# A decoder trunk whose MLPs use seven block products: engine work and weight sums in another order

## Chip, cores, metric

One core of one Trainium2 chip runs the whole program in one launch. The metric is device time in microseconds, the median of several executions. One further execution is profiled; rows and durations below come from that one.

## What is computed

The reference is a trunk of two blocks over 1040 tokens (16 meta tokens and 1024 real ones), width 1024, float32: differential attention, then gated linear attention, each followed by a squared-ReLU MLP with 4096 hidden units. The change touches the MLPs alone:

```python
def sq_relu_mlp(x, w_up, w_down):
    return jnp.square(jax.nn.relu(x @ w_up)) @ w_down
...
for i in range(DEPTH):
    hn = rmsnorm(h, mix_norm_w[i])
    ...
    h = h + sq_relu_mlp(rmsnorm(h, mlp_norm_w[i]), mlp_w_up[i], mlp_w_down[i])
return rmsnorm(h[:, N_META:], final_norm_w)
```

## The kernel before, in words

Activations lie with features on partitions and tokens along the free axis. A product in float32 accuracy is made of three fp32r matmuls: each operand is split into a high part (a CAST on ACT, line 229) and a low part (a subtraction on DVE, line 230, `split_to`), and high x high, low x high and high x low are summed in PSUM.

Each MLP matrix product is done as a 2 x 2 block product with seven instead of eight block multiplications (numbered 1 to 7) and sums of operand blocks. In layer 0 a token half has 520 columns and takes two PSUM banks of 260; in layer 1 it has 512 columns in one bank.

**The first MLP product** (`mlp`, line 941) goes through 16 steps p of 256 hidden units. For each p two 512 KB tiles of weights (`raw`, line 681) hold the blocks A11, A12 and A21, A22. `sums` (line 961) forms on POOL S1 = A21 + A22 in a tile of the pool "tmp" (line 966), then at once S2 = S1 - A11, S3 = A22 - S2, S4 = A12 - S2 in place (lines 969 to 971). `wop_next` (line 974) splits one weight operand into the next of 11 tiles used in a ring; seven operands are ahead of the product in hand. `product` issues a product's matmuls (`part`, line 1000), 24 of 260 columns in layer 0, 12 of 512 columns in layer 1, in the order 1(p), 4(p-1), 2(p), 3(p-1), 6(p), 5(p), 7(p). Products 1, 6, 7 and 4 of one p add up in one bank group without clearing it, so after each of them `after` (line 1052) has to read the banks: ACT copies after 1, 6 and 7 (lines 1059, 1061, 1063), DVE reads after 4. Bank groups alternate with p. So the copy after 7(p) must be done when 4(p) begins, one product later. `gate` (line 1031) applies relu times the norm's factor on DVE (line 1033) and squares on ACT (line 1034). After product 3, `spill_pair` (line 1036) forms T1 to T4 (DVE, lines 1040 to 1048, tiles of "tmp", which has four buffers) and writes seven operands of the second product to DRAM (`xd`).

**The second MLP product** (`Down`, line 725) takes the seven block products in the order `DORD` = 5, 3, 1, 6, 7, 4, 2, each in 16 steps kp; within a step its four output parts mp take turns (`mul`, line 866; matmul line 872). `make_w` (line 788) loads the weight blocks (line 767), sums them (lines 806, 809 and 816 on POOL, 811 on DVE) and splits them; `make_x` reads `xd` back (line 840) and splits it. The first four of these reads land in "tmp". At a product's last kp `evict` (line 876) adds each bank to the residual tile `hacc` on DVE (line 880). `hacc` is loaded during product 5 (line 898). Layer 0 uses banks 2 mp and 2 mp + 1 for all products; layer 1 uses bank mp for 5, 3 and bank mp + 4 for 1, 6, 7, 4.

The engines' queues are not in the order of the code: the framework's scheduler puts an instruction into its engine's queue when its own model has it ready, and uses the code's order as a priority; each engine then works through its queue in order and waits there on semaphores.

Of the kernel before, what the change touches and what calls it, by code (L numbers as in the profile page):

```python
# [8 lines left out]
F32 = mybir.dt.float32  # L9
# [41 lines left out]
def tile_hybrid_trunk(ctx, tc, hT, win, lamp, wout, gwin, gwz, gwup, gwout, wup, wdn, wdl,  # L51
# [676 lines left out]
    class Down:  # L728
        def __init__(self, layer, op, cfg, xd, hook):
            self.__dict__.update(locals())  # L730
            self.tw, self.ns = cfg.tw, len(cfg.subs)
            self.half = (slice(0, cfg.tw), slice(cfg.tw, 2 * cfg.tw))
            self.acc, self.S, self.W, self.X, self.R, self.st = {}, {}, {}, {}, {}, {}
            self.nr = self.nw = self.nx = self.nd = 0
            self.rawp, self.wp, self.stage = [], 1, None
# [8 lines left out]
            self.xring = list(cfg.os[11:16]) + list(cfg.os[7:11]) + list(cfg.os[:7])  # L744
# [42 lines left out]

        def make_w(self, upto):
            while self.nw < min(upto, len(self.wseq)):
                n = self.nw  # L790
                it = self.wseq[n]
                i = it[0]
                j = it[1] if len(it) == 2 else 4 * it[1] + it[2]
                nr = self.rneed(n)
                self.raw(nr)
                at = self.w_place(n)
                if at is None:
                    self.wp = 1 - self.wp
                    o = wpool.tile([P, KT * P], F32R, tag=("wh", "wl")[self.wp], name=nm("wop"))
                else:  # L800
                    o = slot(at, "wop", F32R, (P, KT * P))
                if i == 5:
                    if j % 2 == 0:
                        self.S[j // 2] = slot(self.cfg.ops[j // 2], "S", F32, (P, 2, 512))
                    src = self.S[j // 2][:, j % 2, :]
                    nc.gpsimd.tensor_add(src, self.raw_of(5, j, "A21"), self.raw_of(5, j, "A22"))  # L806
                elif i == 3:
                    S = self.S[j // 2][:, j % 2, :]
                    nc.gpsimd.tensor_sub(S, S, self.raw_of(3, j, "A11"))
                    src = self.raw_of(3, j, "A12")  # L810
                    nc.vector.tensor_sub(src, src, S)  # L811
                elif i == 6:
                    src = self.S[j // 2][:, j % 2, :]
                elif i == 7:
                    src = self.raw_of(7, j, "A22")
                    nc.gpsimd.tensor_sub(src, src, self.S[j // 2][:, j % 2, :])
# [14 lines left out]
        def dma_x(self, upto):  # L831
            while self.nd < min(upto, 112):
                i, kp = self.xseq[self.nd]
                if self.nd < 4:
                    t = tmp("xr")[:, :self.tw]
                else:
                    if self.stage is None:
                        self.stage = [slot(self.cfg.ops[14 + q], "xr", F32, (P, 2, self.tw)) for q in range(2)]
                    t = self.stage[self.nd // 2 % 2][:, self.nd % 2, :]
                nc.sync.dma_start(t, self.xd[i][kp])  # L840
                self.X[i, kp] = t
                self.nd += 1

        def make_x(self, upto):
            tw = self.tw
            while self.nx < min(upto, 112):
                i, kp = self.xseq[self.nx]
                self.dma_x(self.nx + 1)
                o = slot(self.xring[self.nx % 16], "xop", F32R, (P, 2 * tw))
                split_to(o[:, :tw], o[:, tw:], self.X[i, kp])  # L850
                self.X[i, kp] = o
                self.nx += 1
                if self.nx >= 4 or self.nd < 4:
                    self.dma_x(min(self.nx + 2, 4) if self.nx < 4 else self.nx + 2)
# [20 lines left out]

        def evict(self, i, mp, c0, b, nb, n):
            e, h = INTO[i]
            m = 4 * (1 - e) + mp
            a = self.acc[m][:, h * self.tw + c0:h * self.tw + c0 + nb * n].rearrange("p (s n) -> p s n", s=nb)
            nc.vector.tensor_add(a, PS[:, b:b + nb, :n], a)  # L880

        def run(self):
            ns, subs = self.ns, self.cfg.subs
            t = 0
            for i in DORD[:6]:
                par = 1 if i in (1, 6, 7, 4) else 0
                for kp in range(NP2):
                    self.make_w(t + 6 if t < 72 else t + 4 if t < 92 or ns == 2 else 98 + 2 * (t - 92))
                    self.make_x(t + 6 if t < 80 else t + 6 + (t - 79) // 2)
                    for mp in range(4):  # L890
                        b = 2 * mp if ns == 2 else mp + 4 * par
                        self.mul(i, kp, mp, subs, range(b, b + ns), i in (3, 6, 7, 4))
                        if kp == NP2 - 1:
                            self.evict(i, mp, 0, b, ns, subs[0][1])
                    if i == 5 and 3 <= kp < 11:
                        m = kp - 3
                        self.acc[m] = slot(self.cfg.acc[m], "hacc")
                        nc.sync.dma_start(self.acc[m][:, :2 * self.tw], self.op.hm[m])
                    self.hook(self, i, kp)
                    t += 1  # L900
            if ns == 2:
                for mp in range(4):
                    for kp in range(NP2):
# [4 lines left out]
                        self.mul(2, kp, mp, subs, (2 * mp, 2 * mp + 1), False)  # L908
                        if kp == NP2 - 1:
                            self.evict(2, mp, 0, 2 * mp, 2, subs[0][1])  # L910
                        self.hook(self, 2, 16 * mp + kp)
            else:
                for s in range(2):
                    sub = [(256 * s, 256)]
                    for j in range(64):
# [4 lines left out]
                        self.mul(2, kp, mp, sub, (4 * s + mp,), False)  # L920
                        if kp == NP2 - 1:
                            self.evict(2, mp, 256 * s, 4 * s + mp, 1, 256)
# [6 lines left out]
    def up_order(layer):  # L929
# [11 lines left out]
    def mlp(layer, op, cfg, hook):  # L941
# [10 lines left out]
        make = [x for x in make if x[1] < 2] + [(i, p) for p in range(2, NP2) for i in (1, 2, 6, 5, 7, 4, 3)]  # L952
# [8 lines left out]
        def sums(p, name):  # L961
            r0, r1 = get_raw(p)
            a11, a12, a21, a22 = r0[:, :512], r0[:, 512:], r1[:, :512], r1[:, 512:]
            if (p, "S1") not in S:
                S[p, "S1"] = tmp("S1")[:, :512]
                nc.gpsimd.tensor_add(S[p, "S1"], a21, a22)  # L966
            if name != "S1" and (p, "S2") not in S:
                S[p, "S3"], S[p, "S2"], S[p, "S4"] = a21, a11, a12
                nc.gpsimd.tensor_sub(a11, S[p, "S1"], a11)
                nc.gpsimd.tensor_sub(a21, a22, a11)  # L970
                nc.gpsimd.tensor_sub(a12, a12, a11)  # L971
            return S[p, name]

        def wop_next():
# [10 lines left out]
            if i == 1 and p + 1 < NP2:  # L985
                get_raw(p)
                get_raw(p + 1)
            r0, r1 = get_raw(p)
# [6 lines left out]
            wops[i, p] = o  # L995

# [55 lines left out]
        def after(i, p):  # L1052
# [24 lines left out]
            if i == 3:  # L1077
                spill_pair(p)
# [9 lines left out]
        for kp in range(4):  # L1088
            for i, p in lead:
                product(i, p, kp, kp + 1)  # L1090
        for i, p in lead:
            wop_next()
            after(i, p)
        last5 = [p for i, p in lead if i == 5]
        ahead = 7
        t = len(lead)
        for x in seq:
# [4 lines left out]
            else:  # L1102
                while made[0] < min(len(make), t + ahead):
                    wop_next()
                product(*x)
                after(*x)
                t += 1
                if t >= 7 * NP2 - 8:
                    dn.lead(t - 7 * NP2 + 8)
        used[0] += NP2  # L1110
# [329 lines left out]
    def hook1(dn, i, k):  # L1440
# [7 lines left out]
        elif i == 2:  # L1448
# [12 lines left out]
            if k == 127:  # L1461
                fin1(256, 256, 1)
# [84 lines left out]
```

## Time and profile before

| | us |
|---|---|
| median of 3 runs (2453.32 to 2456.03) | 2454.81 |
| the profiled execution | 2455.46 |
| its span | 2453.7 |
| first MLP product, layer 0 (line 1000) | from 607 to 961 |
| second MLP product, layer 0 (line 872) | from 954 to 1296 |
| first MLP product, layer 1 | from 1780 to 2121 |
| second MLP product, layer 1 | from 2115 to 2442 |

The stretches overlap by a few matmuls, because the second product's first matmuls stand before the first product's last ones. Times in rows count from the span's start. "Idle before" is the time an engine stood still before an instruction, with what released it; PE is the matmul stream, DVE, ACT and POOL are the vector, scalar and GpSimd engines.

### The profile page before, as it was taken

Reading aid. Unit: us, or ns where it says so; the run is one execution under the profiler, and the core shown is the slowest. Engines: PE = TensorE matmul, PEld = TensorE weight load, DVE = VectorE, ACT = ScalarE, POOL = GpSimd, SP = SyncE. Lnnn points to the kernel's source line nnn. Section 1 sums busy time; section 2 is a strip of 40 time slices with the busy share of each in tenths; the row PEclk is TensorE's granted clock in tenths of the full one; section 3 lists DMA queues with packets and bytes.
Section 4 is the critical chain, followed back from the end, with each engine's and each line's share of the span. In section 5 each row is a group of like instructions: output and inputs, shape, how many; then the busy total and the mean of one; then the engine's idle time right before and its main releaser. Section 6 shows DMA issues by size and latency. Waiting matters only on the chain. (4 is left out here: it accounts for less than half of the span.)

```text
span 2453.7 us, 38883 instructions
## 1 busy us (share of the span) xinstructions
PE 2370.0 (97%) x14862; PEld 2164.3 (88%) x14862; DVE 1709.0 (70%) x3448; ACT 1089.6 (44%) x2095; POOL 354.6 (14%) x242
## 2 busy tenths in 40 slices
PE   8999999999899999999999999999999999999998
PEld 8999999999899999999998898898877777778888
DVE  7777777767866676866666576685786666688565
ACT  5555555645433333343443334333553343335442
POOL 0000000001322323511000000000132233352100
PEclk9999999999999999999999999999999999999999
DMA  4122222523333337874551112123343333787453
GB/s 161 51 62 61 62 61 60 191 72 133 126 144 126 139 136 257 309 230 124 156 173 57 35 35 69 35 76 122 137 142 142 132 135 137 256 297 249 146 173 106
DMA packets 130826, 326.15 MB, mean 133 GB/s; under 512 B 14864, under 2 KB 22480, under 8 KB 130640
## 3 DMA queue, kind: packets, MB, share of 16 engines
q1 hardware_dynamic: 130640, 323.68, 39.2%
q8 instruction: 116, 1.90, 0.3%
q14 instruction: 70, 0.57, 0.1%
HBM read 227.43 MB, written 87.67 MB: 128 GB/s over the span
## 5 line engine op out<-in xcount | busy, mean ns | idle before, releaser
L1000 PE MATMUL PS<-xop,wop 128*128 128x260 f32 (+1 forms) x4032 | 646.3, 321 | 44.7 <-ACT C L1063 37.5
L1000 PEld LDWEIGHTS PS<-xop,wop 128*128 128x128 f32 x4032 | 576.4, 189 | 115.0 <-ACT C L1063 46.3
L872 PE MATMUL PS<-xop,wop 128*128 128x260 f32 (+2 forms) x4224 | 642.7, 315 | 14.6 <-DVE hacc L880 7.8
L872 PEld LDWEIGHTS PS<-xop,wop 128*128 128x128 f32 x4224 | 589.6, 190 | 67.2 <-DVE C L1033 6.8
L230 DVE TENSOR_TENSOR wop<-raw,wop 128x512 fp32r<-128x512 f32 x352 | 315.6, 908 | 145.8 <-ACT wop L229 137.1
L229 ACT CAST wop<-raw 128x512 fp32r<-128x512 f32 x352 | 215.1, 620 | 388.0 <-PE PS L1000 89.8
L190 PE MATMUL PS<-xh,wh 128*128 128x346 f32 (+2 forms) x992 | 349.1, 352 | 0.0
L191 PE MATMUL PS<-xh,wl 128*128 128x346 f32 (+2 forms) x992 | 334.8, 338 | 0.4 <-DVE wl L171 0.4
L192 PE MATMUL PS<-xl,wh 128*128 128x346 f32 (+2 forms) x992 | 333.2, 336 | 0.0
L230 DVE TENSOR_TENSOR xop<-xr,xop 128x520 fp32r<-128x520 f32 (+1 forms) x224 | 175.0, 793 | 38.3 <-ACT xop L229 38.3
L190 PEld LDWEIGHTS PS<-xh,wh 128*128 128x128 f32 x992 | 187.6, 189 | 7.9
L192 PEld LDWEIGHTS PS<-xl,wh 128*128 128x128 f32 x992 | 187.3, 189 | 7.9
L191 PEld LDWEIGHTS PS<-xh,wl 128*128 128x128 f32 x992 | 187.3, 189 | 7.8 <-DVE wl L171 0.6
L966 POOL TENSOR_TENSOR S<-raw 128x512 f32<-128x512 f32 x32 | 48.5, 1516 | 869.5 <-DVE xop L230 441.0
L229 ACT CAST xop<-xr 128x520 fp32r<-128x520 f32 (+1 forms) x224 | 137.7, 620 | 64.2 <-DMA xr<-xd 47.7
L1034 ACT ACTIVATE C<-C 128x520 f32<-128x520 f32 (+1 forms) x128 | 81.3, 635 | 177.8 <-DVE C L1033 177.7
L429 ACT ACTIVATE e<-e,mx 128x16 f32<-128x16 f32 (+5 forms) x144 | 105.8, 736 | 87.4 <-DVE mx L428 86.1
L230 DVE TENSOR_TENSOR wop<-S,wop 128x512 fp32r<-128x512 f32 x96 | 98.0, 1025 | 64.8 <-ACT wop L229 62.5
L170 ACT CAST wh<-raw 128x1024 fp32r<-128x1024 f32 (+2 forms) x64 | 65.2, 1018 | 155.9 <-PE PS L192 145.3
L191 PE MATMUL PS<-oh,wl 128*128 128x512 f32 (+2 forms) x320 | 112.8, 352 | 0.8 <-DVE wl L171 0.8
L192 PE MATMUL PS<-ol,wh 128*128 128x512 f32 (+2 forms) x320 | 112.9, 353 | 0.0
L190 PE MATMUL PS<-oh,wh 128*128 128x512 f32 (+2 forms) x320 | 112.3, 354 | 0.0
(243 smaller groups left out, 3307.4 us busy)
## 6 DMA issues: line engine op xcount, KB each, us to landing
raw<-in_wdn_dram SPq DMA_DIRECT2D x120, 512.0 KB, 4.7
raw<-in_wup_dram SPq DMA_DIRECT2D x64, 512.0 KB, 3.7
xr<-xd SPq DMA_DIRECT2D x112, 260.0 KB, 3.6
xr<-xd SPq DMA_DIRECT2D x112, 256.0 KB, 3.6
xd<-T SPq DMA_DIRECT2D x64, 260.0 KB, 2.3
xd<-T SPq DMA_DIRECT2D x64, 256.0 KB, 2.2
xd<-C SPq DMA_DIRECT2D x48, 260.0 KB, 2.2
raw<-in_gwin_dram SPq DMA_DIRECT2D x24, 512.0 KB, 3.5
```

Source lines behind the costliest of these rows:

```text
L170: nc.scalar.copy(wh[:, :w], raw[:, :w])
L190: nc.tensor.matmul(ps[:, :n], wh[:, w0:w0 + P], xh[:, c0:c0 + n], start=j == 0, stop=False)
L191: nc.tensor.matmul(ps[:, :n], wl[:, w0:w0 + P], xh[:, c0:c0 + n], start=False, stop=False)
L192: nc.tensor.matmul(ps[:, :n], wh[:, w0:w0 + P], xl[:, c0:c0 + n], start=False, stop=j == len(xs) - 1)
L229: nc.scalar.copy(hi, src)
L230: nc.vector.tensor_sub(lo, src, hi.bitcast(F32))
L429: nc.scalar.activation(e[c][:, :nk], e[c][:, :nk], AF.Exp, bias=nmx[:, c:c + 1], accum_out=sums[:, c, i:i + 1])
L872: nc.tensor.matmul(PS[:, b, :n], W[:, wo + wc:wo + wc + P], X[:, xo + c0:xo + c0 + n], start=kp == 0 and q == 0 and not more, stop=kp == N ...
L966: nc.gpsimd.tensor_add(S[p, "S1"], a21, a22)
L1000: nc.tensor.matmul(ps[:, :n], o[:, wi + kp * P:wi + (kp + 1) * P], xi[:, c0:c0 + n], start=start and q == 0, stop=stop and q == 2, skip_gr ...
L1034: nc.scalar.activation(C[p][e][:, half], C[p][e][:, half], AF.Square)
```

## The change

In `Down`: product order 5, 1, 6, 7, 3, 4, 2 with another bank map; A11 is loaded once, not twice; after 5's (and in layer 0 after 7's) last matmuls ACT copies the banks to "tmp" and DVE adds the copies to `hacc` later (`add_kept`); product 3 no longer adds on 5's banks in layer 0, nor 4 on 7's; all subtractions of weight sums are on POOL, started up to one weight ahead (`sum_w`); `hacc` is loaded in halves during products 1 and 6; the first four reads of `xd` have their own tile; operands are made after a step's matmuls.

```diff
-    DORD = (5, 3, 1, 6, 7, 4, 2)
+    DORD = (5, 1, 6, 7, 3, 4, 2)
-    WSRC = {5: ("A21", "A22"), 3: ("A11", "A12"), 1: ("A11",), 6: (), 7: ("A22",), 4: ("A22",), 2: ("A12",)}
+    WSRC = {5: ("A21", "A22"), 1: ("A11",), 6: (), 7: ("A22",), 3: ("A12",), 4: ("A22",), 2: ("A12",)}
...
+            if self.ns == 2:
+                self.more = {6, 7}
+                self.kept = {5: ((1, 1), (0, 1)), 7: ((1, 1), (1, 0))}
+            else:
+                self.more = {6, 7, 3, 4}
+                self.kept = {5: ((1, 1),)}
...
+        def bank(self, i, mp):
+            if self.ns == 2:
+                return (0, 4, 2, 6)[mp]
+            return ((0, 2, 6, 7), (1, 3, 4, 5))[i in (1, 6, 7, 4)][mp]
...
+        def sum_w(self, upto):
+            while self.nsum < min(upto, 80):
...
+                elif i in (7, 3):
+                    src = self.raw_of(i, j, WSRC[i][0])
+                    nc.gpsimd.tensor_sub(src, src, self.S[j // 2][:, j % 2, :])
...
+                self.sum_w(n + 2)
...
-                elif i == 3:
-                    S = self.S[j // 2][:, j % 2, :]
-                    nc.gpsimd.tensor_sub(S, S, self.raw_of(3, j, "A11"))
-                    src = self.raw_of(3, j, "A12")
-                    nc.vector.tensor_sub(src, src, S)
...
+                if i == 1:
+                    S = self.S[j // 2][:, j % 2, :]
+                    nc.gpsimd.tensor_sub(S, S, src)
...
         def evict(self, i, mp, c0, b, nb, n):
+            if i in self.kept:
+                t = tmp("ev")[:, :self.tw]
+                nc.scalar.copy(t.rearrange("p (s n) -> p s n", s=nb), src)
+                self.adds += [(t, e, mp, h) for e, h in self.kept[i]]
+                return
...
+                    if self.adds and i in (1, 3) and kp >= (6 if i == 1 else 2):
+                        self.add_kept()
```

In `mlp`: S1 replaces A21 in place; each of S1 to S4 is a request of its own, made right after the split that frees its tile; the next pair of weight tiles is requested after operand 2 instead of 1; operands 4 and 7 change places in the making order; a square is written one product later and the spill two products later in the code; layer 1 has another order of the first products.

```diff
-            seq = [(6, 0), "rs0", (6, 1), "rs1", (7, 0), (7, 1), (4, 0), (3, 0)]
+            seq = [(6, 0), "rs0", (7, 0), "rs1", (4, 0), (3, 0), (6, 1), (7, 1)]
...
-        make = [x for x in make if x[1] < 2] + [(i, p) for p in range(2, NP2) for i in (1, 2, 6, 5, 7, 4, 3)]
+        make = [x for x in make if x[1] < 2] + [(i, p) for p in range(2, NP2) for i in (1, 2, 6, 5, 4, 7, 3)]
...
-                S[p, "S1"] = tmp("S1")[:, :512]
-                nc.gpsimd.tensor_add(S[p, "S1"], a21, a22)
...
+            if (p, name) not in S:
+                if name == "S1":
+                    S[p, name] = a21
+                    nc.gpsimd.tensor_add(a21, a21, a22)
...
+            if i == 1:
+                sums(p, "S2")
+            elif i == 5:
+                sums(p, "S3")
+            elif i == 6:
+                sums(p, "S4")
+            elif (i, p) == (3, 0):
+                get_raw(2)
+            elif i == (7 if p > 1 else 4) and 0 < p < NP2 - 1:
+                sums(p + 1, "S1")
...
-            nc.scalar.activation(C[p][e][:, half], C[p][e][:, half], AF.Square)
+            h = C[p][e][:, half]
+            due.append((t + 1, lambda: nc.scalar.activation(h, h, AF.Square)))
...
-                spill_pair(p)
+                due.append((t + 2, lambda: spill_pair(p)))
+            settle(t)
```

## Rows read from the trace of the kernel before

**Rows 1.** The page, part 1: each engine's busy time, share, instructions.
```profile
PE 2370.0 (97%) x14862; PEld 2164.3 (88%) x14862; DVE 1709.0 (70%) x3448; ACT 1089.6 (44%) x2095; POOL 354.6 (14%) x242
```
**Rows 2.** Waits of PE: line, released by; us in total, times, longest.
```profile
PE PS L1000 <- ACT C L1063: 37.5, 27, 1.8
...
PE PS L872 <- DVE hacc L880: 7.8, 5, 3.3
PE PS L872 <- DVE C L1033: 6.2, 2, 3.9
```
**Rows 3.** Six stretches: us, busy us (x instructions) by engine, clock, DMA share, GB/s.
```profile
650.00:950.00 300.00, 283.13 (x2323) 280.25 (x2322) 205.87 (x248) 114.45 (x194) 91.39 (x60) 0.99 0.39 141
950.00:1100.00 150.00, 141.65 (x1134) 140.25 (x1134) 112.82 (x143) 63.42 (x112) 50.09 (x34) 0.97 0.82 281
1100.00:1250.00 150.00, 150.00 (x1254) 150.00 (x1253) 87.94 (x128) 67.66 (x118) 11.68 (x8) 1.00 0.48 144
1850.00:2100.00 250.00, 231.01 (x986) 184.04 (x984) 170.77 (x211) 96.92 (x163) 78.34 (x50) 1.00 0.38 136
2100.00:2200.00 100.00, 93.48 (x397) 75.05 (x396) 73.50 (x90) 37.52 (x66) 45.03 (x29) 0.98 0.83 296
2200.00:2350.00 150.00, 150.00 (x651) 122.08 (x650) 102.78 (x142) 69.47 (x122) 27.16 (x19) 1.00 0.61 195
```
**Rows 4.** Four short stretches, PE alone: us, busy us (x), clock, DMA share, GB/s.
```profile
742.00:750.00 8.00, 8.00 (x57) 0.79 0.58 198
963.00:972.00 9.00, 8.28 (x44) 0.62 0.78 289
1063.00:1068.00 5.00, 4.13 (x23) 0.66 0.46 145
2125.00:2130.00 5.00, 4.42 (x13) 0.66 1.00 361
```
**Rows 5.** ACT in order of time, one step of layer 1's first product.
```profile
1921.83 0.62 ACT L229 CAST wop<-S 128x512 fp32r<-128x512 f32 x1
1923.62 0.62 ACT L229 CAST wop<-raw 128x512 fp32r<-128x512 f32 x1 [1.17 <-POOL raw L969]
1925.33 0.62 ACT L229 CAST wop<-raw 128x512 fp32r<-128x512 f32 x1 [1.08 <-POOL raw L970]
1927.02 0.62 ACT L229 CAST wop<-raw 128x512 fp32r<-128x512 f32 x1 [1.07 <-POOL raw L971]
1927.55 0.58 ACT L1063 COPY C<-PS 128x512 f32<-128x512 f32 x1
```
**Rows 6.** POOL in order of time, the same step.
```profile
1920.50 1.29 POOL L966 TENSOR_TENSOR S<-raw 128x512 f32<-128x512 f32 x1 [14.82 <-DVE T L1048]
...
1925.26 1.73 POOL L971 TENSOR_TENSOR raw<-raw 128x512 f32<-128x512 f32 x1
```
**Rows 7.** PE in order of time, the same step, and layer 0's start.
```profile
1928.18 17.15 PE L1000 MATMUL PS<-xop,wop 128*128 128x512 f32 x73 [1.59 <-ACT C L1063]
...
622.32 3.15 PE L1000 MATMUL PS<-xop,wop 128*128 128x260 f32 x24 [0.69 <-ACT C L1061]
```
**Rows 8.** ACT in order of time, end of layer 1's first product.
```profile
2123.58 0.62 ACT L229 CAST xop<-xr 128x512 fp32r<-128x512 f32 x1 [6.03 <-DMA xr<-xd]
```
**Rows 9.** Groups by line: busy us, mean ns | idle before, released by.
```profile
L811 DVE TENSOR_TENSOR raw<-raw,S 128x512 f32<-128x512 f32 x32 | 34.6, 1116 | 1.2 <-POOL S L809 1.2
L816 POOL TENSOR_TENSOR raw<-raw,S 128x512 f32<-128x512 f32 x32 | 47.1, 1492 | 188.3 <-DMA raw<-in_wdn_dram 147.7 <-DVE xop L230 37.9 <-DVE hacc L880 2.7
L880 DVE TENSOR_TENSOR hacc<-PS,hacc 128x520 f32<-128x520 f32 (+2 forms) x60 | 36.2, 650 | 17.7 <-PE PS L872 17.7
```
**Rows 10.** DVE in order of time, the step of rows 5.
```profile
1922.49 1.66 DVE L230 TENSOR_TENSOR wop<-S,wop 128x512 fp32r<-128x512 f32 x1
...
1928.88 0.68 DVE L230 TENSOR_TENSOR wop<-raw,wop 128x512 fp32r<-128x512 f32 x1
```
**Rows 11.** DMA issues: kind, count, KB each, median us to landing.
```profile
raw<-in_wup_dram SPq DMA_DIRECT2D x64, 512.0 KB, 3.7
```

More of the change, by code (lines that the diff above doesn't have):

```diff
@@ L734, in __init__ @@
             self.nr = self.nw = self.nx = self.nd = 0
-            self.rawp, self.wp, self.stage = [], 1, None
+            self.rawp, self.wp, self.stage, self.nsum, self.adds = [], 1, {}, 0, []
+            if self.ns == 2:
[4 more added lines that the diff above has]
+                self.kept = {5: ((1, 1),)}
             steps = [(i, kp) for i in DORD for kp in range(NP2)]
@@ L786, in w_place @@
             return None
+        def sum_w(self, upto):
+            while self.nsum < min(upto, 80):
+                n = self.nsum
+                i, j = self.wseq[n]
+                if n > self.nw and i in (5, 7, 3) and self.rneed(n) > self.nr:
+                    return
+                if i in (5, 7, 3):
+                    self.raw(self.rneed(n))
+                if i == 5:
+                    if j % 2 == 0:
+                        self.S[j // 2] = slot(self.cfg.ops[j // 2], "S", F32, (P, 2, 512))
+                    nc.gpsimd.tensor_add(self.S[j // 2][:, j % 2, :], self.raw_of(5, j, "A21"),
+                                         self.raw_of(5, j, "A22"))
+                elif i in (7, 3):
+                    src = self.raw_of(i, j, WSRC[i][0])
+                    nc.gpsimd.tensor_sub(src, src, self.S[j // 2][:, j % 2, :])
+                self.nsum += 1
         def make_w(self, upto):
@@ L833, in dma_x @@
                 i, kp = self.xseq[self.nd]
-                if self.nd < 4:
-                    t = tmp("xr")[:, :self.tw]
-                else:
-                    if self.stage is None:
-                        self.stage = [slot(self.cfg.ops[14 + q], "xr", F32, (P, 2, self.tw)) for q in range(2)]
-                    t = self.stage[self.nd // 2 % 2][:, self.nd % 2, :]
+                n = self.nd
+                if n < 4:
+                    at, v = self.cfg.os[14], n % 2
+                else:
+                    at, v = self.cfg.ops[14 + n // 2 % 2], n % 2
+                if at not in self.stage:
+                    self.stage[at] = slot(at, "xr", F32, (P, 2, self.tw))
+                t = self.stage[at][:, v, :]
                 nc.sync.dma_start(t, self.xd[i][kp])
@@ L852, in make_x @@
                 self.nx += 1
-                if self.nx >= 4 or self.nd < 4:
-                    self.dma_x(min(self.nx + 2, 4) if self.nx < 4 else self.nx + 2)
+                self.dma_x(self.nx + (1 if self.nx < 4 else 2))
         def lead(self, k):
@@ L874, in mul, with part, add_kept, load_acc @@
                                      skip_group_check=more)
+        def part(self, e, mp, h, c0=0, n=None):
+            c0 += h * self.tw
+            return self.acc[4 * (1 - e) + mp][:, c0:c0 + (n or self.tw)]
         def evict(self, i, mp, c0, b, nb, n):
[L877 to L880, printed above, removed]
+            src = PS[:, b:b + nb, :n]
+            if i in self.kept:
+                t = tmp("ev")[:, :self.tw]
+                nc.scalar.copy(t.rearrange("p (s n) -> p s n", s=nb), src)
+                self.adds += [(t, e, mp, h) for e, h in self.kept[i]]
+                return
+            a = self.part(*(INTO[i][0], mp, INTO[i][1]), c0, nb * n).rearrange("p (s n) -> p s n", s=nb)
+            nc.vector.tensor_add(a, src, a)
+        def add_kept(self):
+            t, e, mp, h = self.adds.pop(0)
+            a = self.part(e, mp, h)
+            nc.vector.tensor_add(a, a, t)
+        def load_acc(self, m, h):
+            if m not in self.acc:
+                self.acc[m] = slot(self.cfg.acc[m], "hacc")
+            nc.sync.dma_start(self.acc[m][:, self.half[h]], self.op.hm[m][:, self.half[h]])
         def run(self):
@@ L885, in run @@
             for i in DORD[:6]:
-                par = 1 if i in (1, 6, 7, 4) else 0
                 for kp in range(NP2):
+                    for mp in range(4):
+                        b = self.bank(i, mp)
+                        self.mul(i, kp, mp, subs, range(b, b + ns), i in self.more)
+                        if kp == NP2 - 1:
+                            self.evict(i, mp, 0, b, ns, subs[0][1])
+                    if i == 1 and kp < 8:
+                        self.load_acc((kp // 2) + 4 * (kp % 2), 1)
+                    elif i == 1 and kp < 12:
+                        self.load_acc(kp - 4, 0)
+                    elif i == 6 and kp < 4:
+                        self.load_acc(kp, 0)
+                    if self.adds and i in (1, 3) and kp >= (6 if i == 1 else 2):
+                        self.add_kept()
+                    self.hook(self, i, kp)
+                    t += 1
                     self.make_w(t + 6 if t < 72 else t + 4 if t < 92 or ns == 2 else 98 + 2 * (t - 92))
                     self.make_x(t + 6 if t < 80 else t + 6 + (t - 79) // 2)
[L890 to L900, printed above, removed]
             if ns == 2:
@@ L907, in run @@
                             self.make_x(96 + kp + 8)
-                        self.mul(2, kp, mp, subs, (2 * mp, 2 * mp + 1), False)
+                        b = self.bank(2, mp)
+                        self.mul(2, kp, mp, subs, (b, b + 1), False)
                         if kp == NP2 - 1:
-                            self.evict(2, mp, 0, 2 * mp, 2, subs[0][1])
+                            self.evict(2, mp, 0, b, 2, subs[0][1])
                         self.hook(self, 2, 16 * mp + kp)
@@ L919, in run @@
                             self.make_x(96 + kp + 8)
-                        self.mul(2, kp, mp, sub, (4 * s + mp,), False)
+                        b = self.bank((2, 4)[s], mp)
+                        self.mul(2, kp, mp, sub, (b,), False)
                         if kp == NP2 - 1:
-                            self.evict(2, mp, 256 * s, 4 * s + mp, 1, 256)
+                            self.evict(2, mp, 256 * s, b, 1, 256)
                         self.hook(self, 2, 64 * s + j)
@@ L963, in sums @@
             a11, a12, a21, a22 = r0[:, :512], r0[:, 512:], r1[:, :512], r1[:, 512:]
-            if (p, "S1") not in S:
-                S[p, "S1"] = tmp("S1")[:, :512]
-                nc.gpsimd.tensor_add(S[p, "S1"], a21, a22)
[L967 to L971, printed above, removed]
+            if (p, name) not in S:
+                if name == "S1":
+                    S[p, name] = a21
+                    nc.gpsimd.tensor_add(a21, a21, a22)
+                elif name == "S2":
+                    S[p, name] = a11
+                    nc.gpsimd.tensor_sub(a11, a21, a11)
+                elif name == "S3":
+                    S[p, name] = a21
+                    nc.gpsimd.tensor_sub(a21, a22, a11)
+                else:
+                    S[p, name] = a12
+                    nc.gpsimd.tensor_sub(a12, a12, a11)
             return S[p, name]
@@ L984, in wop_next @@
                 o = slot(t, "wop", F32R, (P, KT * P))
-            if i == 1 and p + 1 < NP2:
-                get_raw(p)
+            r0, r1 = get_raw(p)
+            if i == 1:
+                sums(p, "S1")
+            elif i == 2 and p != 1 and p + 1 < NP2:
                 get_raw(p + 1)
-            r0, r1 = get_raw(p)
             name = PROD[i][0]
@@ L995, in wop_next @@
             wops[i, p] = o
+            if i == 1:
+                sums(p, "S2")
[7 more added lines that the diff above has]
+                sums(p + 1, "S1")
         def part(ps, o, x, c0, n, kp, start, stop, more):
@@ L1077, in after, with settle @@
             if i == 3:
-                spill_pair(p)
+                due.append((t + 2, lambda: spill_pair(p)))
+            settle(t)
+        due = []
+        def settle(now):
+            ready = [d for d in due if d[0] <= now]
+            due[:] = [d for d in due if d[0] > now]
+            for _, d in ready:
+                d()
         pend, rs_done = [], [False]
@@ L1090, in mlp @@
                 product(i, p, kp, kp + 1)
+        t = 0
         for i, p in lead:
+            after(i, p)
             wop_next()
-            after(i, p)
-        last5 = [p for i, p in lead if i == 5]
         ahead = 7
         t = len(lead)
+        while made[0] < t + ahead:
+            wop_next()
         for x in seq:
@@ L1102, in mlp @@
             else:
-                while made[0] < min(len(make), t + ahead):
-                    wop_next()
                 product(*x)
@@ L1107, in mlp @@
                 t += 1
+                while made[0] < min(len(make), t + ahead):
+                    wop_next()
                 if t >= 7 * NP2 - 8:
                     dn.lead(t - 7 * NP2 + 8)
+        settle(t + 2)
         used[0] += NP2
@@ L1461, in hook1 @@
             if k == 127:
-                fin1(256, 256, 1)
+                fin1(256, 256, 2)
                 for m in range(KT):
```

12 lines of the change are left out of this document (2 added, 10 removed).

## The prediction

> **What bounds the kernel now.** I read the page first: PE is busy 97% of the span, POOL 14%, ACT 44%, DVE 70% [rows 1]. So the kernel is PE's stream of matmuls and the places where that stream stops. The waits of PE come next: of the listed waits in the two MLPs, 37.5 us in 27 stops end with ACT's copy at line 1063, and 14.0 us in 7 stops end with DVE at lines 880 and 1033 [rows 2]. All of them lie where this change works.
>
> The waits view shows less than a stop costs, because ends of matmuls are modelled. I therefore count matmuls by stretch. Unstopped, layer 0 does 1254 in 150 us, 119.6 ns each, and layer 1 does 651 in 150 us, 230.4 ns each [rows 3]. At these rates the 2323 matmuls of 650 to 950 us need 277.9 of 300 us: **22.1 lost**. The 986 of 1850 to 2100 us need 227.2 of 250: **22.8 lost**. The 1134 of 950 to 1100 us need 135.6 of 150: **14.4 lost**; the 397 of 2100 to 2200 us need 91.5 of 100: **8.5 lost**. Part of that is clock: in four short stretches right behind a stop the granted clock averages 0.79, 0.62, 0.66 and 0.66, so PE ran partly at the lower of its two levels, 1.2 GHz [rows 4]. In full-speed time that is 8 x 0.21 = 1.7, 9 x 0.38 = 3.4 and twice 5 x 0.34 = 1.7 us, 8.5 in all; 1.7 of it lies in the first 22.1 us and 3.4 + 1.7 in the 14.4, 1.7 in the 8.5.
>
> **Why the 27 stops happen.** In one step of layer 1 [rows 5 to 7] PE has finished 7(p) and 1(p+1) and stops for 1.59 us ahead of 4(p), until 1928.18 [rows 7]. The copy it needs ran from 1927.55 to 1928.13 [rows 5]. The copy does not wait for PE; in ACT's queue it stands behind four casts, three of which wait for POOL's sums of lines 969, 970 and 971 [rows 5]. POOL is not slow on average: it stood idle 14.82 us before S1, waiting for DVE's T4 at line 1048, since S1 needs a tile of "tmp" that the spill of the step before still holds; from there its four sums run back to back, 1920.50 to 1926.99 [rows 6]. So one shared buffer makes POOL late, POOL blocks ACT, and ACT's copy stops PE. The written order is not the cause: the casts in the bunch belong to products of different turns of the loop.
>
> **The change, part by part.**
>
> *Sums in place and early.* S1 no longer takes a tile of "tmp" and each sum is requested when its own tile is free, so POOL's 6.5 us of sums can start up to 14.8 us earlier [rows 6]. What replaces the stop: S3 now overwrites S1, so it comes after the split of operand 5. That serial piece is a cast of 0.62 [rows 5], a DVE split of 0.68 to 1.66 [rows 10], a sum of 1.73 [rows 6] and the next cast, 0.62: 3.7 to 4.6 us. The copy after 6(p) may queue behind it and is wanted one product later, which gives it 12 x 0.230 = 2.8 us more. Operand 5(p+1) goes into the ring's tile that 3(p-1) gives back, just as 6(p) begins, so the piece starts one product (2.8 us) ahead of that copy's turn, and 5.5 us stand against 3.7 to 4.6 plus the copy's 0.58. It fits with 0.3 to 1.2 us to spare. By the stretches a stop costs (22.1 - 1.7) / 14 = 1.46 us in layer 0 (14 stops lie in it) and 22.8 / 12 = 1.90 in layer 1, where a thirteenth lies ahead of the stretch: 22.1 + 22.8 + 1.9 = 46.8 us are to be had. Bounds: all of it, or half of it (the margin is used up). I take 41, leaving 0.2 us a stop for steps where a copy still meets a late cast, because the margin is nearer to enough than to nothing.
>
> *Squares and spill later.* A square waits for DVE's gate. Written one product later it cannot stand ahead of a copy that is ready, but no square stands between rows of the bunch [rows 5], so it gains nothing there: 0. The spill's seven writes on SP's queue start up to two products later; what it frees is wanted by 1(p+2), two products after that, so the cover is 5.5 us against four subtractions of 0.7. If it were gone, the copy at line 1059 would wait, and its bank has three products to spare. The next weights are requested one operand later on SP and take 3.7 us to land [rows 11]; their first sum comes four operands later, 11 us: 0.
>
> *Banks of product 5, its operands, its loads.* Product 5 in layer 1 moves off banks 1, 3 and 5, which the last products of the first MLP half use, and in layer 0 it comes to their banks last; this removes the stops on line 1033, 2.3 and 3.9 us [rows 2]. Before one of them ACT had sat 6.03 us on a read of `xd` into a "tmp" tile [rows 8]; those reads get a tile of their own. With the clock behind the stops, 3.4 and 1.7 [rows 4], this part holds 11.3 us. I take 9: the first weights, with 3.7 us to land [rows 11] and more under a DMA share of 0.82 [rows 3], may put a short wait in its place. Bounds: 4 and 11.3.
>
> *Second product 1 instead of 3.* DVE loses 32 subtractions of 1.12 us and POOL gets 32 of 1.49 [rows 9]; sixteen 512 KB loads go, and the loads of `hacc` move out of product 5, where the DMA share was 0.82. The stops on line 880 come from a DVE queue filled with splits whose weights are late: five stops, 7.8 us [rows 2], with refill and a clock spell some 10.3 (14.4 + 8.5 less the 11.3 above and 1.3 unassigned). I take half, 5.5, since the new copies out of the banks stand on ACT, which waits for the same weights. Bounds: 0 and 10.3. The added work: 12 copies on ACT at 0.58 [rows 5] in place of 12 evictions of 0.65 on DVE [rows 9], and 20 additions of tiles at about 0.7: 14 us of DVE, less than the 35.7 that leave it, spread over two products. Cost 0; if DVE were full they would lengthen those two products by at most 14.
>
> *Layer 1's first products.* 6(0), 7(0) and 4(0) now follow each other on one bank with only a norm matmul between. Layer 0 had that order and shows a stop of 0.69 for such a copy [rows 7]. Two such places, with refill: cost 1.5; bounds 0 and 4.
>
> **Sum.** 41 + 9 + 5.5 - 1.5 = 54, against the profiled execution's 2455.46 (span 2453.7 and 1.8 around it; 0.65 above the median of 2454.81): **2401 us**. All upper bounds: 46.8 + 11.3 + 10.3 = 68, 2387. All lower ones: 23 + 4 + 0 - 4 = 23, 2432.
>
> **Where a page speaks against it.** In the same step a split beside POOL's sums took 1.66 us and one without them 0.68 [rows 10]. The Trainium skill, page "SBUF — State Buffer", section "SBUF: two separate sides", says that a DVE instruction with two SBUF inputs and a GpSimd instruction that reads SBUF take an exclusive lock, and the other one is blocked for the whole instruction; the trace agrees, 1.66 being 0.68 and most of a sum. By that rule, sums that no longer run in one clump meet more splits, each late by up to one sum; the serial piece above would then stand at its long end in every step, and 2420, the first rival's time, would be the result.
>
> **Rivals.** *First: the stop moves.* The copy after 6(p) takes the place of the copy after 7(p) behind a cast that waits for S3. For it: the margin is 0.3 us with the 1.66 split. Against it: POOL has far more idle time than work. Price: 0.9 us (between the 0.2 taken and a full stop) in 27 steps, so the sums gain 46.8 - 24.3 = 22.5 and the whole 22.5 + 9 + 5.5 - 1.5 = 35.5: 2420. Chance 0.18.
>
> *Second: the change does not reach the queues.* The scheduler sets their order, so the bunch of casts could form again around another cause and the 27 stops stay. Then only the other parts count, 13: 2442. Against it: S1's wait for "tmp" is removed by name, not by order. Chance 0.05.
>
> *Third, the slower side: the weights become a loop of their own.* A pair of weight tiles is loaded again only when its last split is done; with S1 in place, its sums and splits are chained: 3.7 landing [rows 11], four sums of 1.3 to 1.7, seven splits of 0.62 + 0.68 to 1.66, some 22 us in all, plus the time a split waits until the ring of 11 tiles has a free one. A step is now 84 x 0.230 + 1.9 = 21.3 us, two are 42.6. It makes the kernel's first MLP halves slower from the point where the ring adds over 20.6 us. Two us beyond that, every step takes 22.3 instead of 21.3, over 27 steps 27 us more than now, less the other parts' 13: 2469. For it: such waits for PE stood ahead of casts already. Against it: the ring is freed at PE's own pace, and POOL would have to be late by products, not by 1 us. Chance 0.06.
>
> A further 0.03 is for gains and costs that cancel.
>
> **Numbers.** Forecast 0.68, first rival 0.18, second 0.05, none 0.03, third 0.06. Range 2387 to 2432: the forecast's own bounds, which also hold the first rival; the others, 0.14, are left out. A change under 0.2%, 4.9 us, could not be told from none. Faster 0.91, same 0.03, slower 0.06.
>
> **What would show it.** Right: no line 1063 among PE's waits over 5 us; POOL's S1 without a wait for line 1048; 650 to 950 us near 2480 matmuls; clock 1.00 in the first half. First rival: PE's waits headed by the copy of line 1061. Second: line 1063 as before. Third: PE waiting for casts of operands, line 229. For the second half: no wait on line 1033 at its start, and waits on line 880 halved, or ACT's new copies in their place. The forecast is wrong if PE, no longer stopped, still does fewer than 1254 in 150 us.

## The result, and the profile after

The changed kernel takes **2425.18 us** (median of 4 runs, 2423.38 to 2427.14) against 2455.31 for the kernel before in the same comparison: ratio 0.9879, 95% interval 0.9862 to 0.9896. That is 30 us faster; 54 were forecast, and 2425 lies in the stated range. The profiled execution has a span of 2421.6 us.

The waits of PE after the change (line, released by; us in total, times, longest) answer to [rows 2]. Lines have moved: 1000 is now 1062, 1063 is 1126, 872 is 894, 880 is 910; 1124 is the copy after 6, 906 the new copy out of the banks.

```profile
PE PS L894 <- ACT ev L906: 9.7, 1, 9.7
...
PE PS L1062 <- ACT C L1124: 6.3, 3, 5.1
PE PS L894 <- DVE hacc L910: 5.0, 1, 5.0
PE PS L1062 <- ACT C L1126: 3.2, 2, 1.8
```

The 27 stops on the copy after 7(p) are gone, two late ones are left, and the stops on line 1033 no longer appear. In their place stand three long single stops, 5 to 10 us each. POOL's S1 no longer waits for the spill, but for once (POOL's waits, the kernel before and then the changed one; line 1111 was 1048):

```profile
POOL S L966 <- DVE T L1048: 243.0, 16, 17.2
```
```profile
POOL raw L1013 <- DVE T L1111: 12.6, 1, 12.6
```

The stretches (columns as in [rows 3]) show where:

```profile
650.00:930.00 280.00, 280.00 (x2339) 280.00 (x2338) 164.91 (x246) 110.46 (x190) 80.07 (x57) 1.00 0.44 152
932.00:1080.00 148.00, 136.84 (x1130) 136.23 (x1129) 103.22 (x130) 65.69 (x115) 55.12 (x35) 0.97 0.70 229
...
1800.00:2050.00 250.00, 250.00 (x1082) 202.71 (x1081) 160.66 (x234) 104.40 (x182) 70.41 (x50) 1.00 0.44 152
2080.00:2180.00 100.00, 95.67 (x412) 76.87 (x410) 81.62 (x92) 49.70 (x88) 51.88 (x34) 1.00 0.85 282
```

In the middle of the first MLP products PE is busy for the whole of 280 and 250 us, at 119.7 and 231 ns a matmul: the unstopped rates of [rows 3]. Around 932 to 1080 us it is not. Three short stretches (PE alone: us, busy us, clock, DMA share, GB/s) answer to [rows 4]; behind each long stop the granted clock falls again:

```profile
984.00:1004.00 20.00, 10.33 (x76) 0.74 0.87 293
1784.00:1800.00 16.00, 10.92 (x36) 0.79 0.22 87
2170.00:2195.00 25.00, 19.97 (x75) 0.86 0.54 172
```

In full-speed time that is 20 x 0.26 = 5.2, 16 x 0.21 = 3.4 and 25 x 0.14 = 3.5 us. So the stop at 988 us costs about 15, the one at 1785 and the one at 2177 about 9 each.

For the account I cut the trace at the first and last matmul of the two MLP lines (us). A first product ends here where its last matmul starts, and the second one is counted from there:

| | first, layer 0 | second, layer 0 | first, layer 1 | second, layer 1 |
|---|---|---|---|---|
| before | 352.9 | 335.8 | 341.1 | 320.6 |
| after | 335.9 | 333.2 | 327.6 | 320.9 |

The first products are 30.5 us shorter, the second ones 2.3. Nearly all that was won was won in the first half.

**How the three long stops come about.** The one at 988 us lies between products 5 and 1 of layer 0. POOL, DVE, ACT and PE of the changed kernel, in order of time, one fence each:

```profile
972.39 13.78 POOL L840 TENSOR_TENSOR S<-S,raw 128x512 f32<-128x512 f32 x8 [0.48 <-DMA raw<-in_wdn_dram]
```
```profile
976.42 1.78 DVE L230 TENSOR_TENSOR wop<-raw,wop 128x512 fp32r<-128x512 f32 x1
978.13 3.50 DVE L230 TENSOR_TENSOR xop<-xr,xop 128x520 fp32r<-128x520 f32 x2
981.55 3.47 DVE L230 TENSOR_TENSOR wop<-raw,wop 128x512 fp32r<-128x512 f32 x2
...
991.85 0.68 DVE L230 TENSOR_TENSOR wop<-raw,wop 128x512 fp32r<-128x512 f32 x1
```
```profile
987.87 1.25 ACT L229 CAST xop<-xr 128x520 fp32r<-128x520 f32 x2 [7.00 <-DMA xr<-xd]
...
997.27 2.06 ACT L906 COPY ev<-PS 128x520 f32<-128x520 f32 x4
```
```profile
997.90 3.33 PE L894 MATMUL PS<-xop,wop 128*128 128x260 f32 x15 [9.67 <-ACT ev L906]
```

Read from the top: POOL runs eight of the subtractions S - A11 without a gap. They are not new: the kernel before has the same 32 on POOL, in product 3 and in pairs (997 to 1041 us in layer 0):

```profile
L809 POOL TENSOR_TENSOR S<-S,raw 128x512 f32<-128x512 f32 x32 | 54.6, 1728 | 37.8 <-DMA raw<-in_wdn_dram 27.0 <-DVE raw L811 4.5 <-DVE hacc L880 3.7
```

New is their place, in one piece while PE is still in product 5. Beside them each split on DVE takes 1.75 us, and 0.68 without them. The raw tiles come free late, and SP's queue stands on a raw load; its own waits for 970 to 1000 us say by how much:

```profile
SPq L778 <- DVE wop L230: 13.6, 3, 6.5
SPq L863 <- DVE xop L230: 8.4, 8, 3.0
```

Behind that load wait the reads of `xd`; ACT stands 7.00 us on one of them, and the four copies out of product 5's banks stand behind ACT's casts, until 997.27. PE had been done since 988.

The stop at 2177 us (end of product 1, layer 1) has DVE's eviction at its end, behind splits whose casts waited for `xd` (the last time for 3.46 us, until 2174.32). POOL had run ten of the same sums without a gap from 2116.7 to 2133.3. That this stop hangs on them is shown by e6 and e11 below, where it is gone. The one at 1785 us is ACT's copy after 6(0), behind a cast that waits 7.30 us for POOL's S2:

```profile
1789.88 0.62 ACT L229 CAST wop<-raw 128x512 fp32r<-128x512 f32 x1 [7.30 <-POOL raw L1016]
1790.40 0.58 ACT L1124 COPY C<-PS 128x512 f32<-128x512 f32 x1
```

### The profile page after: what moved, and what is told of

It reads as the page before. It is cut to its first block, busy times and chain, and to the rows that moved or that the text cites. A ratio compares the mean times of both kernels' runs of the same rounds, so it can differ in the third digit from the quotient of the medians.

```text
span 2421.6 us, 38887 instructions
## 1 busy us (share of the span) xinstructions
PE 2366.2 (98%) x14862; PEld 2164.7 (89%) x14862; DVE 1656.2 (68%) x3424; ACT 1091.9 (45%) x2107; POOL 387.3 (16%) x274
## 4 chain that ended last, share of the span: by engine, by line
PE 82%; DVE 8%; DMA 4%; issue 2%; ACT 2%; POOL 1%; SPq 0%; DVEq 0%; POOLq 0%; ACTq 0%
PE PS L1062 22%; PE PS L894 21%; PE PS L190 9%; PE PS L192 9%; PE PS L191 8%; DMA xr<-xd 3%; PE PS L469 2%; DVE wop L230 2%; DVE xop L230 1%; PE PS L453 1%; PE PS L1374 1%; DMA raw<-in_wdn_dram 1%; PE PS L422 1%; PE PS L421 1%; PE PS L220 1%
## 5 line engine op out<-in xcount | busy, mean ns | idle before, releaser
L230 DVE TENSOR_TENSOR wop<-raw,wop 128x512 fp32r<-128x512 f32 x384 | 302.1, 793 | 219.4 <-ACT wop L229 218.8
L229 ACT CAST wop<-raw 128x512 fp32r<-128x512 f32 x384 | 234.8, 620 | 344.7 <-PE PS L894 79.4
L230 DVE TENSOR_TENSOR xop<-xr,xop 128x520 fp32r<-128x520 f32 (+1 forms) x224 | 194.2, 877 | 41.4 <-ACT xop L229 41.2
L1013 POOL TENSOR_TENSOR raw<-raw 128x512 f32<-128x512 f32 x32 | 46.6, 1456 | 543.7 <-DMA raw<-in_wup_dram 526.3
L815 POOL TENSOR_TENSOR raw<-raw,S 128x512 f32<-128x512 f32 x64 | 96.6, 1530 | 172.2 <-DMA raw<-in_wdn_dram 154.7
```

What stands on the lines that cost most here:

```text
L229: nc.scalar.copy(hi, src)
L230: nc.vector.tensor_sub(lo, src, hi.bitcast(F32))
```

## Experiments

Times are medians; ratios are to the kernel before in the same comparison (2454.4 to 2458.2 us), each with its 95% interval.

**One half at a time (e1, e2).** `class Down` from the one kernel, `mlp` from the other.

> The kernel before with the changed first MLP products alone (sums in place and early, squares and spill later, layer 1's new first order); the second products as before. Theory: the 27 stops on the copy after 7(p) cost 46.8 us and go with the sums, and layer 1's new first order gives some 9 us back, so the time is about 2418 and the first MLP stretches last as long as with the whole change (336 and 328 us), while the stops on DVE at the start of the second products stay. Rival: the second products' change is what shortens the kernel; then this one stays within 5 us of 2455.

> The kernel before with the changed second MLP products alone. Theory: they gain nothing by themselves, because the stops on DVE (some 18 us with the clock behind them) come back as stops behind ACT's copies and DVE's evictions: 2450 to 2460, with the 27 stops on the copy after 7(p) in place. Rival: they gain their forecast 14 us and lose it only in company of the changed first products: about 2441.

e1: 2418.72 us, 0.9847 (0.9833 to 0.9862). e2: 2463.72 us, 1.004 (1.0025 to 1.0055). The first half alone is ahead of the whole change; the second half alone is slower than before, and above the theory's 2450 to 2460. In e2 the 28 stops on the copy stand as before, and the stops of the second products are all there:

```profile
PE PS L1045 <- ACT C L1108: 37.5, 28, 2.2
PE PS L894 <- ACT ev L906: 10.2, 1, 10.2
PE PS L894 <- ACT xop L229: 9.0, 1, 9.0
```

e1 shows more: it has the old bank map, and yet no wait on line 1033. Those stops went with the first half.

**Layer 1's first order (e3), squares and spill (e4).** Both are the whole change with one part undone, e3 the first pair of lines, e4 the others:

```diff
-            seq = [(6, 0), "rs0", (7, 0), "rs1", (4, 0), (3, 0), (6, 1), (7, 1)]
+            seq = [(6, 0), "rs0", (6, 1), "rs1", (7, 0), (7, 1), (4, 0), (3, 0)]
...
-            due.append((t + 1, lambda: nc.scalar.activation(h, h, AF.Square)))
+            nc.scalar.activation(h, h, AF.Square)
...
-                due.append((t + 2, lambda: spill_pair(p)))
+                spill_pair(p)
```

> The whole change, with layer 1's first products in the order of before: 6(0), 6(1), 7(0), 7(1), 4(0), 3(0). Theory: the stop of 5.9 us at 1785 us, behind a cast that waits for POOL's S2 of the next p, and the clock spell after it (3.4 us) come from the new order: about 2417. Rival: the stop comes from the sums' requests, which stay: 2425 within 3.

> The whole change, but squares and spill written where they were before. Theory: a square or a spill written later gains nothing, because the queues are ordered by readiness: 2425 within 4. Rival: bank reads come first because of it: without it the stops on copies return, 10 us or more: above 2435.

e3: 2420.25 us, 0.9853 (0.9837 to 0.987); e4: 2422.7, 0.9869 (0.9852 to 0.9885). In e3 the cast still waits 6.56 us for S2, but PE now does 6(1) meanwhile and stops for 1.77; layer 1's first product is 321.6 us long, 6.0 less than with the change. The time falls by 4.9, not by 8, and the intervals of e3 and of the change overlap: the stretch shows the cost, the time agrees in sign. e4 is the same as the change: writing squares and spill later is worth nothing that can be measured.

**What makes the 27 stops (e5, e9, e12).** e5 is the kernel before with this alone:

```diff
-            T1, T2, T3, T4 = [tmp("T")[:, :tw] for _ in range(4)]
+            T1, T2, T4 = [tmp("T")[:, :tw] for _ in range(3)]
+            T3 = C0[:, g]
```

> The kernel before, with one edit: T3 of the spill is written over the half of C0 that nobody reads afterwards, so that a step takes four tiles of the pool with four buffers (three T and S1) and not five. The sums' code, their order and everything else stay. Theory: POOL is late because S1 waits for the spill's tile, so S1 no longer waits for T4, POOL's sums start earlier and most of the 27 stops on the copy after 7(p) go: 2410 to 2420. Rival: the sums must also be requests of their own; with the four in one bunch the stops stay: above 2445.

**2403.58 us**, 0.979 (0.977 to 0.981), below the theory's 2410 to 2420, the lowest median of all kernels run and ahead of the whole change. Nothing of line 1063 (here 1064) is left among PE's waits. One step of it, POOL and then ACT, answers to [rows 5, 6]:

```profile
1909.12 1.64 POOL L966 TENSOR_TENSOR S<-raw 128x512 f32<-128x512 f32 x1 [12.71 <-DVE wop L230]
...
1914.14 1.74 POOL L971 TENSOR_TENSOR raw<-raw 128x512 f32<-128x512 f32 x1
```
```profile
1924.74 0.62 ACT L229 CAST wop<-S 128x512 fp32r<-128x512 f32 x1
1925.27 2.70 ACT L229 CAST wop<-raw 128x512 fp32r<-128x512 f32 x5
1929.81 0.59 ACT L1064 COPY C<-PS 128x512 f32<-128x512 f32 x1 [1.84 <-PE PS L1000]
```

The sums are finished 9 us ahead of the casts, which now run without a wait, and the copy waits for PE and not PE for the copy. S1 starts 15.6 us ahead of its own cast at 1924.74, where it was 1.3 us before (1920.50 and 1921.83, [rows 5, 6]).

e9 and e12 try the reverse: the whole change, with S1 back in a tile of "tmp". In e9 S2 is formed from A21 and not from S1, so S2 to S4 are not the sums that the products need; e12 forms it from S1.

```diff
-                    S[p, name] = a21
-                    nc.gpsimd.tensor_add(a21, a21, a22)
+                    S[p, name] = tmp("S1")[:, :512]
+                    nc.gpsimd.tensor_add(S[p, name], a21, a22)
...
-                    nc.gpsimd.tensor_sub(a11, a21, a11)
+                    nc.gpsimd.tensor_sub(a11, S[p, "S1"], a11)
```

> The whole change, with S1 back in a tile of the pool with four buffers; its request stays early and by itself, and the other three sums stay in place. Theory: the tile's place decides, so S1 waits for a tile of the spill again, POOL is late and the stops on the copy after 7(p) come back: 2445 or more. Rival: the early requests of their own suffice: within 5 of 2425.

> As e9, but S2 is formed from the S1 in the pool's tile, as the sums require; in e9 S2 was formed from A21, so it did not depend on S1 or on the tile at all. Theory: S2, S3 and S4 now wait behind S1 for a tile of the spill, and the stops on the copy after 7(p) come back: 2445 or more. Rival: requests of their own let the sums wait without a bunch of casts in front of the copy, so the tile alone does little: below 2432.

e9: 2422.45 us, 0.9856 (0.9839 to 0.9874), which says little, as S2 did not hang on the tile there. e12: 2421.09, 0.9853 (0.9836 to 0.987): the theory is refuted, and by its time the rival holds. POOL of e12, then ACT:

```profile
1920.21 1.33 POOL L1013 TENSOR_TENSOR S<-raw 128x512 f32<-128x512 f32 x1 [8.42 <-DMA xd<-T]
...
1929.96 1.29 POOL L1022 TENSOR_TENSOR raw<-raw 128x512 f32<-128x512 f32 x1 [5.06 <-DVE wop L230]
```
```profile
1920.19 0.62 ACT L229 CAST wop<-raw 128x512 fp32r<-128x512 f32 x1 [1.66 <-PE PS L1062]
1922.97 0.59 ACT L1126 COPY C<-PS 128x512 f32<-128x512 f32 x1 [2.16 <-PE PS L1062]
...
1931.32 0.62 ACT L229 CAST wop<-S 128x512 fp32r<-128x512 f32 x1 [1.43 <-PE PS L1062]
```

S1 still takes a tile of the pool and still waits for a spill, at the same point of the step as in [rows 6]. But it is the S1 of a later step. Counted from the start of layer 1, the S1 at 1920.50 in the kernel before is the eighth and stands ahead of the seventh copy after 7(p); the S1 at 1920.21 in e12 is the tenth and stands ahead of the eighth copy. The tenth cast of an S tile is the one at 1931.32, 11 us later, where the kernel before has 1.3. So the sums are not late in e12 either; they were asked for earlier, and no cast that waits for POOL stands ahead of the copy. One tile fewer from the pool (e5) and earlier requests with the tile kept (e12) both make the sums early, and either ends the stops; the change does both. Whether another order of the casts in ACT's queue would end them with sums as late as before, no run shows. Which of the changed requests is the one that counts in e12 was not tried.

**What the second half costs (e6, e7, e11, e10).** e6 is the change without `nc.gpsimd.tensor_sub(S, S, src)` for i = 1; it leaves that sum out, so products 6, 7 and 3 use other operands. The edit of e7 and, behind the dots, that of e11, which also has layer 1's first order of before:

```diff
-                nc.scalar.copy(t.rearrange("p (s n) -> p s n", s=nb), src)
+                nc.vector.tensor_copy(t.rearrange("p (s n) -> p s n", s=nb), src)
...
-                    nc.gpsimd.tensor_sub(S, S, src)
+                    nc.vector.tensor_sub(S, S, src)
```

> The whole change without POOL's subtraction S - A11 during product 1 (left out, so 6, 7 and 3 use other operands). Theory: eight such sums in a row double DVE's splits to 1.7 us and hold the raw tiles, SP's queue stands 6.5 us on a raw load with the reads of xd behind it, ACT's casts come late and its copies out of product 5's banks later still; without the sums the stop of 9.9 us at 988 us falls below 4 and the time to 2412 or less. Rival: ACT's place in the queue alone makes the stop: it stays above 8 us and the time within 4 of 2425.

> The whole change with the copies out of the banks of products 5 (and 7 in layer 0) on DVE in place of ACT. Theory: both engines work through the same late casts and splits in order, so the stop at 988 us keeps more than half its 9.9 us: 2418 to 2428. Rival: the copies are late because they stand on ACT; then the stop goes and the time is about 2411.

> The whole change with layer 1's first order of before (2420.3) and S - A11 on DVE in place of POOL, nothing left out. Theory: DVE pays 16 subtractions of 0.7 us a layer and saves the doubled splits beside POOL, so raw tiles come free sooner; the stops at the ends of product 5 and 1 halve: 2410 to 2416. Rival: the sum costs the same wherever it runs, since DVE is what the raw tiles wait for: 2418 or more.

e6: 2412.01 us, 0.9821 (0.9804 to 0.9839), 13 less than the change. The splits of 960 to 988 us (DVE at line 230 alone), the changed kernel and then e6:

```profile
960.00:988.00 28.00, 22.67 (x20) 1.00 0.74 247
```
```profile
960.00:988.00 28.00, 21.07 (x26) 1.00 0.92 319
```

Twenty splits at 1.13 us became 26 at 0.81, and DMA moved 319 instead of 247 GB/s, and SP's queue stood at most 3.3 us on a raw load and not 6.5. The stop on ACT's copy fell to one of 3.7:

```profile
PE PS L891 <- ACT ev L903: 3.7, 1, 3.7
```

The stop at the end of product 1 in layer 1 is no longer among the waits.

e7: 2428.02, 0.9882 (0.9867 to 0.9898), the same as the change within its interval; the stop stays, now on DVE, at 11.5 us. It does not matter on which engine the copy stands: both queues hold the late reads of `xd` in front of it.

e11 leaves nothing out: 2407.16, 0.9793 (0.9777 to 0.9808), below its theory's 2410 and 13 below e3, from which it differs by the engine of one subtraction. The pages of e3 and e11 (part 1) say where the time went:

```profile
PE 2365.0 (98%) x14862; PEld 2163.6 (89%) x14862; DVE 1658.7 (69%) x3424; ACT 1091.6 (45%) x2107; POOL 389.6 (16%) x274
```
```profile
PE 2363.4 (98%) x14862; PEld 2163.5 (90%) x14862; DVE 1650.3 (69%) x3456; ACT 1091.1 (45%) x2107; POOL 335.2 (14%) x242
```

DVE took over 32 subtractions and is busy 8.4 us less. Its second products, 330.2 and 312.9 us, are the shortest of all kernels that leave nothing out. Layer 0 keeps a stop of 6.4 us on ACT's copy; in layer 1 none is left there.

> The kernel before with T3 in place (2403.6) and, of the second products' change, the bank map alone. Theory: the stops on line 1033 and 1073 at the second products' start (3.4 us, less a matmul each) go, the others stay: 2399 to 2403. Rival: what waited for banks waits for operands then: 2403 to 2407.

The edit of e10 is e5 with the banks (0, 4, 2, 6) in layer 0 and (0, 2, 6, 7), (1, 3, 4, 5) in layer 1. A bank at the end of the program moves with them. It gives 2406.93, 0.9791 (0.9774 to 0.9809), no gain over e5 (0.979), as the rival had it: line 1033 (here 1035) is gone from the waits and line 880 grows from 5.3 us in e5 to 10.7.

**The parts without cost (e8).** `mlp` of the change with layer 1's old first order, `Down` of before:

> The first MLP products of the change with layer 1's first order of before, and the second products of before: the two parts that cost something left out. Theory: 2418.7 less the 4.9 that the order of before gave in the whole change, 2414. Rival: the stops at the second products' start grow by what is saved ahead of them: 2418 or more.

2412.17, 0.9818 (0.9802 to 0.9835), near the theory's 2414. e3 and e11 have the same first half, so the changed second half by itself costs 8 us here (e3, 2420.25), and with S - A11 on DVE it is 5 us ahead (e11, 2407.16; the intervals of e8 and e11 overlap). e5 is still ahead: its first products are 331.9 and 317.2 us long, those of e8 334.4 and 319.9.

e5's first half and e11's second half were not run together; by their stretches, 331.9 + 330.2 + 317.2 + 312.9 against 331.9 + 332.1 + 317.2 + 316.7, some 6 us below e5 would be the estimate.

## Why the prediction was right, and where it was not

*The sums, 41 of 46.8 us: right, and a little low.* The middle of both stretches reaches the unstopped rate, so nearly all of the 46.8 came. The margin reckoned for the copy after 6(p) held, and the first rival's stops did not appear there. The part of the reason on POOL is shown: in e5 one tile fewer is taken from the pool, S1 comes 15.6 us ahead of its cast and not 1.3, and the stops are gone. "The written order is not the cause" does not stand: in e12 S1 keeps its tile, and earlier requests alone end the stops.

*Squares and spill, 0: right* (e4).

*Banks and first operands of product 5, 9 us: wrong in its cause.* The stops on line 1033 went, but they go in e1 without the bank map too, and e10 with the map gains nothing. With the map alone the wait on line 880 grew in its place.

*Second product 1 instead of 3, 5.5 us: the step that failed.* It counted the 32 subtractions A12 - S that leave DVE, and the loads. For S - A11 it had no term, since POOL forms it before and after. But with product 1 in second place these sums run in one piece at the end of product 5: a split beside them takes 1.75 us in place of 0.68, and the raw tiles, SP's queue and ACT's casts are late in turn. The price is 13 us, by e6 without the sum and by e11 with the sum on DVE. What the 32 moved subtractions cost on POOL was not measured by itself. Doubled splits were in [rows 10], and the page was weighed, but for the first products. The Trainium skill, page "SBUF — State Buffer", section "SBUF: two separate sides", names the exclusive lock between a DVE instruction with two SBUF inputs and a GpSimd one that reads SBUF; where sums run without a gap the trace agrees, 1.75 being 0.68 and most of a sum. In the first products, where the prediction feared it, the sums now stand apart, and DVE's 246 instructions of 650 to 930 us take 164.9 us, where 248 took 205.9 [rows 3]. The other term of that step, the loads of `hacc` moved out of product 5, shows no gain: from 976.9 to 983.4 us SP's queue stood, and the DMA share of 980 to 990 us was 0.55, so DMA was not the limit there.

*Layer 1's first products, 1.5 us: wrong size.* A copy of 0.58 was priced; the copy stands behind a cast that waits for S2, so the stop is 5.1 us by the waits and brings a clock spell of 3.4. By e3 it costs 6.0 in the stretch and 4.9 in the time. The bound of 4 was too low.

*The sum.* 54 was forecast, and 30 came. By the stretches the first half gave 30.5. Counted as time between matmul starts beyond the unstopped rate, the first products lost 46.0 us before and 2.0 after, their first 45 and last 20 us left out. Of these 44, 7.2 went back at layer 1's start, 4.8 in the last 20 us, where the first product hands over to the second (lines 1124 and 1126 at 931, 936, 2077 and 2083 us), and 1.4 at layer 0's start, where 635 to 640 us now has a clock of 0.66. The second half gave 2.3, where 14.5 was forecast. The rivals' mechanisms did not occur; the time is near the first rival's for another reason. That it lies in the range is in part luck: the second half came out below its bounds, and layer 1's start cost more than its bound of 4, and the range held them because its lower end allowed for half of the sums to fail, which they did not.

## What to carry to other kernels

When a busy engine stops at regular places, follow the chain to the first instruction that is late, and ask what it waits for: here one buffer too few in a shared pool (four for five tiles a step) stood behind 27 stops, and writing one tile in place was worth more than the reordering. A copy that frees a bank should not stand in a queue behind work that waits for another engine; here it was enough to make that work early, by a tile fewer or by an earlier request. Compare a late sum with its own consumer, not with the nearest one in time: two kernels can have it at the same point of the step and mean different steps. Work on an idle GpSimd is not free when it runs in one piece beside VectorE, and when a reordering gathers such work, the queues that wait for VectorE's tiles, SP's included, have to be priced.

## What was not expected

The halves nearly add up: e1 gains 36 us, e2 loses 9, the two together gain 30. That one half of the change costs time by itself was not in the prediction. The size of the jam was a surprise too: eight sums of 1.7 us on an engine that is busy 16% of the span led to a stop of 9.7 us and, at the lower clock behind it, 5.2 more; without them a stop of 3.7 is left (e6).
